# Mixer output projection: three weight chunks loaded and gated ahead, LayerNorm in two fused steps, and a fixed VectorE order

## The chip, the core and the metric

One core of one Trainium2 chip runs the whole program. Its engines are TensorE (PE), with a separate row for its weight loads (PEld), VectorE (DVE), ScalarE (ACT), GpSimd (POOL) and SyncE (SP), which issues nearly all transfers. The metric is device microseconds for one execution of the program. Three executions of the kernel before took 984.68, 987.9 and 989.28 us; the median is 987.9 us. A difference under about 0.5%, some 5 us, can't be told from no change with a measurement of this kind.

## What is computed

One layer of a hybrid encoder on 512 tokens of 1024 channels, all in float32. The part that matters here is the seam between the token mixer and the feed-forward network:

```python
    merged = gates[:, :, 0] * y_a + gates[:, :, 1] * y_b + gates[:, :, 2] * y_c
    return merged @ w_o
    ...
        y = _token_mixer(h, ...)
        x = _layer_norm(ALPHA * x + gt_t[:, None, :] * y) * ln_t_g[l] + ln_t_b[l]
        h = _modulate(x, sh_f, sc_f)      # _layer_norm(x) * (1 + sc_f) + sh_f
        y = _conv_ffn(h, w_up[l], conv_w[l], conv_b[l], w_down[l])
        x = _layer_norm(ALPHA * x + gt_f[:, None, :] * y) * ln_f_g[l] + ln_f_b[l]
```

Between the product with `w_o` and the first product with `w_up` there are thus two LayerNorms, one after the other, each over the 1024 channels of a token. The first has a gain and a bias per channel; the second has the adaptive scale and shift. The products need float32 accuracy. The kernel gets it by writing each operand as a high part and a low part (`...h` and `...l`) and multiplying three times: low by high, high by low, high by high.

## The kernel before

Every weight chunk has to be split before TensorE can use it: ScalarE casts it to the high part, and VectorE subtracts that from the raw chunk for the low part. Activations are split the same way.

**Merges.** `merge(2, m)`, for m from 0 to 7, adds the last branch's product to the merged activations: 24 matmuls on PE, a product with the gate on DVE (`th`, L408), the addition on POOL (`mg`, L411), then ACT casts the high half (`mgh`, L1079) and DVE subtracts for the low half (`mgl`, L1080). A merged tile is free for other use once its `mgl` is made.

**Output projection** (`project_out`). The tokens lie in four tiles t of 128 rows and the 1024 output channels in two halves n of 512, so there are eight accumulators `pyo`. The contraction has eight chunks k of `w_o`, named `o0` to `o7`. Chunks 0 and 1 are streamed through all eight accumulators (L1127 to L1130). Chunks 2 to 7 are resident: `scaled_chunk` loads one, POOL multiplies both halves with the gate row `gt` (L1096), ACT casts (L1107) and DVE makes the low half (L1108); only then the matmuls (L106 to L108) go tile by tile, so that `pyo` of t = 0 is complete first. In all 192 matmuls of 512 columns.

**Between the products** (`after_mixer(t)`, called as tile t is complete). The input tile has been loaded into `xr`. DVE adds ALPHA times it to `pyo` (L1180) and takes statistics of each half (L1183) and their aggregate `mv` (L142). POOL makes the reciprocal deviation `rs` in three small steps (`pw` L130, `rs` L133 and L145). ACT applies mean and deviation (L1187), then POOL (half 0) and DVE (half 1) apply gain and bias in two steps each (L1193, L1194). That is the first LayerNorm. Then come statistics again (L1207, L142), the small steps on POOL, and ACT writes the normalized tile to `xr` (L1214). PE turns pairs of tiles (`pth`, L1226; tp = 0 is tokens 0 to 255, tp = 1 tokens 256 to 511), and `second_modulation` applies scale and shift and splits: `h2f` and an even `h2T..h` on ACT (L1234, L1243), an odd one on DVE (L1238), the low parts on DVE (L1246).

**First part of the up-projection** (`up_early`). Six chunks of `w_up` are split in advance (`early_split`, `early_low`: `uph`/`upl` and `wuph`/`wupl` at L1160 and L1166). Their products with tokens 0 to 255 (`pzu`, 256 columns, 144 matmuls) run first, then those with tokens 256 to 511 (144 more), and after that the loop over the other 38 chunks (L113 to L116).

**What sets the order.** The program is written with tile pools, which set the waits; a scheduler places each engine's instructions by its own timeline of the program, and each engine then runs its list strictly in that order. `tc.issue_after` adds an order that data don't need; before, it keeps some steps behind marked ones (`marks`, `after`).

## Time and profile before

| | us |
|---|---|
| three executions | 984.68, 987.9, 989.28 |
| the profiled execution | 988.41 |
| its span, first to last instruction | 986.6 |
| PE busy in the span | 961.1 |
| DVE, ACT, POOL busy | 594.0, 393.8, 311.3 |
| mean clock granted to TensorE | 0.991 of full |
| first `pyo` matmul, last `pyo` matmul | 556.38, 601.70 |
| first `pzu` matmul on tokens 0 to 255 | 610.84 |
| first `pzu` matmul of the loop over the other chunks | 650.58 |

The times of the last three rows count from the start of the span. In a row of the timeline stand the start, the duration, engine, line, operation, the tiles written and read, and how many instructions the row holds; brackets give the idle time of the engine just before and the instruction that ended it. Matmuls are pipelined, so the distance between two starts tells their cost and not the duration. In a row of stretches stand the busy time of PE, PEld, DVE, ACT and POOL with the number of instructions, the clock granted, the share of the DMA engines and GB/s.

### The profile page before, as it was taken

How to read it: one execution, taken by the hardware profiler on the slowest of the kernel's cores; microseconds unless marked ns; L12 is line 12 of the kernel's file. 1: busy time of each engine (PE TensorE's matmuls, PEld its weight loads, DVE VectorE, ACT ScalarE, POOL GpSimd, SP SyncE). 2: the span in 40 equal slices, each digit the busy share in tenths (PEclk: the TensorE clock that was granted, in tenths of full speed). 3: DMA queues.
4: the chain of work that ended last, by engine and by line, in shares of the span. 5: the costliest groups of instructions: out<-in, count | busy, mean ns of one | idle time of the engine just before them, and what ended most of it. 6: DMA issues, size and time to landing. Idle time of an engine off the chain costs nothing.

```text
span 986.6 us, 12263 instructions
## 1 busy us (share of the span) xinstructions
PE 961.1 (97%) x4566; PEld 805.5 (82%) x4566; DVE 594.0 (60%) x891; ACT 393.8 (40%) x658; POOL 311.3 (32%) x311
## 2 busy tenths in 40 slices
PE   8999999999999999999999997999999999999996
PEld 7878888888878888888888876988888888888885
DVE  6967556556685565655533577685565665632367
ACT  4574646543333322522332335464444444422121
POOL 3773111122350031200012746321111121755654
PEclk9999999999999999999999997999999999999999
DMA  9722112144445533363232471133433342343222
GB/s 339 275 67 77 36 54 81 35 132 157 133 128 186 181 123 98 128 224 107 64 107 86 125 259 43 44 128 107 129 107 128 109 145 88 113 123 107 85 86 86
DMA packets 45275, 119.20 MB, mean 121 GB/s; under 512 B 5280, under 2 KB 8736, under 8 KB 45216
## 3 DMA queue, kind: packets, MB, share of 16 engines
q1 hardware_dynamic: 44784, 118.25, 36.9%
q8 instruction: 36, 0.59, 0.3%
q10 hardware_dynamic: 432, 0.17, 0.1%
q14 instruction: 23, 0.19, 0.1%
HBM read 116.30 MB, written 2.10 MB: 120 GB/s over the span
## 4 chain that ended last, share of the span: by engine, by line
PE 79%; DVE 8%; DMA 4%; POOL 4%; ACT 2%; issue 2%; DVEq 0%; SPq 0%; POOLq 0%; ACTq 0%
PE pzu L114 7%; PE pzu L113 7%; PE pzu L116 7%; PE pg L113 4%; PE py L113 4%; PE pg L116 3%; PE pg L114 3%; PE py L114 3%; PE py L116 3%; PE pyd L1127 3%; PE pyd L1130 3%; PE pyd L1129 3%; PE pu L933 3%; PE pu L930 3%; PE pu L932 3%; DVE acc L295 3%
## 5 line engine op out<-in xcount | busy, mean ns | idle before, releaser
L93 DVE TENSOR_TENSOR wupl<-wup,wuph 128x1024 fp32r<-128x1024 f32 x38 | 48.3, 1272 | 71.2 <-PE pzu L116 45.3
L1096 POOL TENSOR_TENSOR d<-d,gtfb 128x512 f32<-128x512 f32 x44 | 73.6, 1694 | 38.3 <-DMA d<-in_wdn 35.9
L1369 POOL TENSOR_TENSOR zc<-zc 128x512 f32<-128x512 f32 x22 | 29.7, 1350 | 173.7 <-ACT zc L1368 130.8
L411 POOL TENSOR_TENSOR mg<-mg,th 128x512 f32<-128x512 f32 x16 | 31.3, 1958 | 144.2 <-DVE th L408 144.0
L1101 DVE TENSOR_TENSOR dl<-d,dh 128x1024 fp32r<-128x1024 f32 x18 | 29.5, 1636 | 55.6 <-PE pyd L1127 50.7
L92 ACT CAST wuph<-wup 128x1024 fp32r<-128x1024 f32 x38 | 39.9, 1050 | 46.5 <-PE pzu L114 46.5
L92 ACT CAST wbh<-wb 128x1024 fp32r<-128x1024 f32 x24 | 25.3, 1054 | 69.3 <-PE py L114 52.6
L93 DVE TENSOR_TENSOR wgl<-wg,wgh 128x1024 fp32r<-128x1024 f32 x22 | 27.0, 1229 | 41.5 <-ACT wgh L92 29.3
L810 DVE SCALAR_TENSOR_TENSOR ada<-adar,cact,ada 128x512 f32<-128x512 f32 x56 | 49.7, 917 | 0.8 <-DMA adar<-in_ada 0.8
L1100 ACT CAST dh<-d 128x1024 fp32r<-128x1024 f32 x18 | 19.0, 1053 | 62.5 <-PE pyd L1130 37.6
L1351 ACT ACTIVATE zc<-pzu,cols 128x512 f32<-128x512 f32 x44 | 34.2, 779 | 22.0 <-PE pzu L116 17.3
L92 ACT CAST wgh<-wg 128x1024 fp32r<-128x1024 f32 x22 | 23.3, 1057 | 38.9 <-PE pg L114 25.2
L93 DVE TENSOR_TENSOR wsgl<-wsg,wsgh 128x1024 fp32r<-128x1024 f32 x16 | 19.6, 1225 | 31.8 <-ACT wsgh L92 26.2
L93 DVE TENSOR_TENSOR wbl<-wb,wbh 128x1024 fp32r<-128x1024 f32 x24 | 30.5, 1269 | 9.7 <-ACT wbh L92 5.5
L92 ACT CAST wsgh<-wsg 128x1024 fp32r<-128x1024 f32 x16 | 16.9, 1053 | 48.7 <-PE pu L933 44.1
L1354 DVE SCALAR_TENSOR_TENSOR zc<-pzu,cols,zc 128x511 f32<-128x511 f32 x44 | 32.6, 743 | 3.9 <-ACT zc L1351 3.9
L731 POOL TENSOR_SCALAR pe<-pe,mx 128x128 f32<-128x128 f32 (+3 forms) x32 | 17.0, 534 | 56.2 <-DVE mx L730 55.8
L1358 DVE SCALAR_TENSOR_TENSOR zc<-pzu,cols,zc 128x510 f32<-128x510 f32 x44 | 32.6, 745 | 0.8
L1096 POOL TENSOR_TENSOR o<-o,gttb 128x512 f32<-128x512 f32 x16 | 26.4, 1674 | 16.6 <-DMA o<-in_wo 13.7
L1368 ACT ACTIVATE zc<-zc 128x512 f32<-128x512 f32 x22 | 13.9, 631 | 40.5 <-DVE zc L1358 40.4
L863 POOL TENSOR_TENSOR asum<-apad 128x527 f32<-128x527 f32 x8 | 12.2, 1519 | 55.4 <-ACT apad L858 29.3
L408 DVE SCALAR_TENSOR_TENSOR th<-th,py 128x512 f32<-128x512 f32 x16 | 11.0, 686 | 30.9 <-PE py L116 30.9
(1430 smaller groups left out, 3170.4 us busy)
## 6 DMA issues: line engine op xcount, KB each, us to landing
wup<-in_wup SPq DMA_DIRECT2D x44, 512.0 KB, 3.6
adar<-in_ada SPq DMA_DIRECT2D x64, 256.0 KB, 3.9
wb<-in_wb SPq DMA_DIRECT2D x24, 512.0 KB, 3.6
wg<-in_wg SPq DMA_DIRECT2D x22, 512.0 KB, 3.6
d<-in_wdn SPq DMA_DIRECT2D x22, 512.0 KB, 3.6
wsg<-in_wsg SPq DMA_DIRECT2D x16, 512.0 KB, 3.7
ada<-in_ada1p SPq DMA_DIRECT2D x24, 256.0 KB, 5.0
wa<-in_wa SPq DMA_DIRECT2D x8, 512.0 KB, 3.5
```

Of the source, the lines that this page charges most:

```text
L92: nc.scalar.copy(out=hi[:, :n], in_=raw[:, :n])
L93: ins = nc.vector.tensor_tensor(out=lo[:, :n], in0=raw[:, :n], in1=f(hi[:, :n]), op=ALU.subtract)
L113: nc.tensor.matmul(o, wh[:, c], xl[k], start=k == 0, stop=False)
L114: nc.tensor.matmul(o, wh[:, c], xh[k], start=False, stop=False)
L116: nc.tensor.matmul(o, wl[:, c], xh[k], start=False, stop=k == KT - 1)
L411: nc.gpsimd.tensor_tensor(out=merged[m], in0=merged[m], in1=th, op=ALU.add)
L810: nc.vector.scalar_tensor_tensor(out=acc[n], in0=src, scalar=cact[:, k : k + 1], in1=acc[n], op0=ALU.mult, op1=ALU.add,)
L1096: nc.gpsimd.tensor_tensor(out=raw[:, c], in0=raw[:, c], in1=gt[n], op=ALU.mult)
L1351: nc.scalar.activation(t, pz, AF.Identity, bias=cols[:, cc + 3 : cc + 4], scale=cols[:, cc + 2 : cc + 3])
L1354: nc.vector.scalar_tensor_tensor(out=t[:, 1:512], in0=pz[:, 0:511], scalar=cols[:, cc + 1 : cc + 2], in1=t[:, 1:512], op0=ALU.mult, op1=AL ...
L1358: nc.vector.scalar_tensor_tensor(out=t[:, 2:512], in0=pz[:, 0:510], scalar=cols[:, cc : cc + 1], in1=t[:, 2:512], op0=ALU.mult, op1=ALU.add,)
L1369: nc.gpsimd.tensor_tensor(out=val, in0=val, in1=gate, op=ALU.mult)
```

## The change

Four things are changed, all between the last merges and the first `pzu` matmuls for tokens 256 to 511.

1. Chunks `o2`, `o3` and `o4` no longer go through `scaled_chunk`'s load. They are loaded as six half tiles (`oraw`) of another pool, and POOL gates one half for each of the first six merges. In the order that the scheduler makes of it, POOL runs these six rows just ahead of its first `mg` addition of the last branch.
2. The input rows are loaded straight into the tiles `x1`, which take the places of the merged tiles as these come free, and all eight loads are issued before the projection; on SP they stand between the weight loads of the merges.
3. The first LayerNorm has two steps on DVE, each with two tensor inputs: `centre` is (x - mean) * gain and `scale` is (that) * rs + bias. The step on ACT and the four on POOL and DVE are gone. POOL still makes `rs`, now in two steps.
4. DVE's steps are chained one behind the other (`in_turn`), from the last low half of `w_o` to the splits for tokens 256 to 511. The low halves of the early `w_up` chunks have fixed places in that chain: chunks 0 to 2 ahead of the first residual, chunk 3 between `centre` and `scale` of t = 0, chunk 4 after the second statistics of t = 1, chunk 5 after those of t = 3. The turns for tokens 0 to 255 stand inside the projection's last matmuls, and for these tokens all high parts are made on ACT.

The diff, cut to its core:

```diff
@@ during the merges
+    o_raw = {}
+    for k in (2, 3, 4):
+        o_raw[k] = [pt_t(f"oraw{k}{n}") for n in range(2)]
+        for n in range(2):
+            nc.sync.dma_start(out=o_raw[k][n], in_=A["wo"][k, :, n * 512 : (n + 1) * 512])
     for m in range(KT):
         merge(2, m, sg_hi, sg_lo, th2.pop(m))
+        if m < 6:
+            raw = o_raw[2 + m // 2][m % 2]
+            nc.gpsimd.tensor_tensor(out=raw, in0=raw, in1=gt_t[m % 2], op=ALU.mult)
@@ project_out
+        if ready:
+            ready()
         for t in range(TT):
             for n in range(2):
                 for k in range(nk - resident, nk):
+                    for work, *args in inside.get((t, n, k), ()):
+                        work(*args)
                     step(t, n, k, ws[k])
             chain(t, acc[t])
@@ the steps between the products
+    def in_turn(work, *args):
+        with ExitStack() as order:
+            for ins in vector_order:
+                order.enter_context(tc.issue_after(ins))
+            vector_order[:] = [work(*args).ins]
+    def centre(t):
+        for n in range(2):
+            ins = nc.vector.scalar_tensor_tensor(
+                out=x1[t][n], in0=x1[t][n], scalar=mv_o[t][:, 0:1], in1=lntg[n],
+                op0=ALU.subtract, op1=ALU.mult,
+            )
+        return ins
+    def scale(t):
+        for n in range(2):
+            ins = nc.vector.scalar_tensor_tensor(
+                out=x1[t][n], in0=x1[t][n], scalar=rs_o[t][:, 0:1], in1=lntb[n],
+                op0=ALU.mult, op1=ALU.add,
+            )
+        return ins
-    def affine(t):
-        for n in range(2):
-            nc.scalar.activation(
-                x1[t][n], x1[t][n], AF.Identity, bias=rs_o[t][:, 1:2], scale=rs_o[t][:, 0:1]
-            )
-    def gain_bias(t):
-        for n, eng in ((0, nc.gpsimd), (1, nc.vector)):
-            eng.tensor_tensor(out=x1[t][n], in0=x1[t][n], in1=lntg[n], op=ALU.mult)
-            eng.tensor_tensor(out=x1[t][n], in0=x1[t][n], in1=lntb[n], op=ALU.add)
+    def weights_ready():
+        vector_order[:] = last_lo
+        for m in range(4):
+            early_split(m)
+        for m in range(3):
+            in_turn(early_low, m, nc.vector)
+    def norm_steps(t, *between):
+        in_turn(residual, t)
+        in_turn(centre, t)
+        for work in between:
+            in_turn(*work)
+        in_turn(scale, t)
     def after_mixer(t, py):
         py_o[t] = py
+        if t < 2:
+            norm_steps(t, *[(early_low, 3, nc.vector)][t:])
+            in_turn(second_stats, t)
+            second_norm(t)
         if t == 1:
+            early_split(4)
+            in_turn(early_low, 4, nc.vector)
         if t == 2:
+            norm_steps(2)
         if t == 3:
+            in_turn(second_modulation, 0, 0)
+            in_turn(second_stats, 2)
+            for jp in (1, 2, 3):
+                in_turn(second_modulation, 0, jp)
+            second_norm(2)
+            early_split(5)
+            norm_steps(3)
+            in_turn(second_stats, 3)
+            second_norm(3)
+            in_turn(early_low, 5, nc.vector)
+    for t in range(TT):
+        x1[t] = [m_t(f"x1_{t}{n}") for n in range(2)]
+        for n in range(2):
+            nc.sync.dma_start(
+                out=x1[t][n], in_=A["x"][t * P : (t + 1) * P, n * 512 : (n + 1) * 512]
+            )
+        {
+            (3, 0, KT - 2): [(turn, 0, 0), (turn, 0, 1)],
+            (3, 1, 3): [(turn, 0, 2)],
+            (3, 1, 5): [(turn, 0, 3)],
+        },
```

How the order moves is seen best at three places. The first is VectorE behind the last low half of `w_o`, that is, where the residual of tile 0 is formed. `x1_00` and `x1_01` are the two halves of tile 0, `x1_10` and `x1_11` those of tile 1, `x1_20` of tile 2; `sto` and `st` hold statistics; `wupl` and `upl` are low halves of early `w_up` chunks. Before:

```order
L1180 SCALAR_TENSOR_TENSOR x1_00_5274<-xr00_5270,pyo_5080 128x512
L1183 BN_STATS sto_5276<-x1_00_5274 128x6
L1180 SCALAR_TENSOR_TENSOR x1_01_5275<-xr01_5271,pyo_5081 128x512
L1180 SCALAR_TENSOR_TENSOR x1_10_5291<-xr10_5287,pyo_5082 128x512
L1166 TENSOR_TENSOR wupl_5310<-wup_5307,wuph_5309 128x512
L1183 BN_STATS sto_5276<-x1_01_5275 128x6
L1166 TENSOR_TENSOR wupl_5310<-wup_5307,wuph_5309 128x512
L1183 BN_STATS sto_5293<-x1_10_5291 128x6
L1180 SCALAR_TENSOR_TENSOR x1_11_5292<-xr11_5288,pyo_5083 128x512
L142 BN_AGGR mv_5298<-sto_5276 128x2
L1166 TENSOR_TENSOR wupl_5394<-wup_5391,wuph_5393 128x512 x2
```

Now:

```order
L1180 TENSOR_TENSOR wupl_5265<-wup_5262,wuph_5264 128x512 x2
L1196 SCALAR_TENSOR_TENSOR x1_00_5098<-x1_00_5098,pyo_5114 128x512
L1196 SCALAR_TENSOR_TENSOR x1_01_5099<-x1_01_5099,pyo_5115 128x512
L1199 BN_STATS sto_5316<-x1_00_5098 128x6
L1199 BN_STATS sto_5316<-x1_01_5099 128x6
L1201 BN_AGGR mv_5321<-sto_5316 128x2
L1208 SCALAR_TENSOR_TENSOR x1_00_5098<-x1_00_5098,mv_5321,lntg0_5074 128x512
L1208 SCALAR_TENSOR_TENSOR x1_01_5099<-x1_01_5099,mv_5321,lntg1_5076 128x512
L1180 TENSOR_TENSOR wupl_5271<-wup_5268,wuph_5270 128x512 x2
L1216 SCALAR_TENSOR_TENSOR x1_00_5098<-x1_00_5098,rs_5323,lntb0_5078 128x512
L1216 SCALAR_TENSOR_TENSOR x1_01_5099<-x1_01_5099,rs_5323,lntb1_5080 128x512
L153 BN_STATS st_5333<-x1_00_5098 128x6
```

Tiles 0 and 1 were interleaved and now follow each other; the low halves of chunk 2 stand ahead of the first residual, those of chunk 3 between `centre` and `scale`, and the gain and bias, which came later from three engines, are these four rows.

The second place is ScalarE ahead of the first split for the up-projection (`h2T0h`, made of the turned tile `pth`; `xr` is the tile that the second LayerNorm writes). Before:

```order
L1160 CAST wuph_5309<-wup_5307 128x512 x2
L1160 CAST wuph_5393<-wup_5391 128x512 x2
L1187 ACTIVATE x1_00_5274<-x1_00_5274,rs_5300 128x512
L1187 ACTIVATE x1_01_5275<-x1_01_5275,rs_5300 128x512
L1187 ACTIVATE x1_10_5291<-x1_10_5291,rs_5368 128x512
L1187 ACTIVATE x1_11_5292<-x1_11_5292,rs_5368 128x512
L1214 ACTIVATE xr00_5270<-x1_00_5274,rs_5384 128x512
L1214 ACTIVATE xr01_5271<-x1_01_5275,rs_5384 128x512
L1214 ACTIVATE xr10_5287<-x1_10_5291,rs_5447 128x512
L1214 ACTIVATE xr11_5288<-x1_11_5292,rs_5447 128x512
L1234 ACTIVATE h2f_5470<-pth_5465,shfc_3497,scfc_4400 128x256
L1243 ACTIVATE h2T0h_5064<-pth_5465,shfc_3497,scfc_4400 128x256
```

Now:

```order
L1174 CAST wuph_5264<-wup_5262 128x512 x2
L1174 CAST wuph_5270<-wup_5268 128x512 x2
L1229 ACTIVATE xr00_5343<-x1_00_5098,rs_5338 128x512
L1229 ACTIVATE xr01_5344<-x1_01_5099,rs_5338 128x512
L1229 ACTIVATE xr10_5408<-x1_10_5102,rs_5403 128x512
L1229 ACTIVATE xr11_5409<-x1_11_5103,rs_5403 128x512
L1174 CAST uph40_5414<-wup_5412 128x512
L1174 CAST uph41_5415<-wup_5412 128x512
L1260 ACTIVATE h2T0h_5082<-pth_5485,shfc_3497,scfc_4400 128x256
L1263 ACTIVATE h2f_5529<-pth_5485,shfc_3497,scfc_4400 128x256
L1260 ACTIVATE h2T1h_5083<-pth_5485,shfc_3497,scfc_4400 128x256
```

The first LayerNorm's four rows (L1187) are gone, and the cast of `w_up` chunk 4 (`uph4`) stands between the second LayerNorm of tile 1 and the first split.

The third place is TensorE at the end of the projection: `pyo` are its accumulators, `pth` the turns, `pzu` the up-projection. Before:

```order
L106 MATMUL pyo_5087<-o7l1_5219,mgh7_5052 128x512
L107 MATMUL pyo_5087<-o7h1_5217,mgl7_5053 128x512
L108 MATMUL pyo_5087<-o7h1_5217,mgh7_5052 128x512
L1226 MATMUL pth_5465<-ident_95,xr00_5270 128x128
L1226 MATMUL pth_5483<-ident_95,xr00_5270 128x128
L1226 MATMUL pth_5495<-ident_95,xr01_5271 128x128
L1226 MATMUL pth_5554<-ident_95,xr01_5271 128x128
L1226 MATMUL pth_5465<-ident_95,xr10_5287 128x128
L1226 MATMUL pth_5465<-ident_95,xr00_5270 128x128
...
L106 MATMUL pzu_5616<-h2T0l_5072,uph00_5262 128x256
L107 MATMUL pzu_5616<-h2T0h_5064,upl00_5264 128x256
```

Now:

```order
L108 MATMUL pyo_5120<-o5h0_5214,mgh5_5002 128x512
L1241 MATMUL pth_5485<-ident_95,xr00_5343 128x128
L1241 MATMUL pth_5490<-ident_95,xr00_5343 128x128
L106 MATMUL pyo_5120<-o6l0_5228,mgh6_5039 128x512
...
L106 MATMUL pyo_5121<-o5l1_5217,mgh5_5002 128x512
L1241 MATMUL pth_5485<-ident_95,xr10_5408 128x128
L1241 MATMUL pth_5485<-ident_95,xr00_5343 128x128
L1241 MATMUL pth_5485<-ident_95,xr10_5408 128x128
...
L108 MATMUL pyo_5121<-o7h1_5239,mgh7_5070 128x512
L106 MATMUL pzu_5610<-h2T0l_5090,uph00_5248 128x256
L107 MATMUL pzu_5610<-h2T0h_5082,upl00_5250 128x256
```

The sixteen turns for tokens 0 to 255 stood behind the last `pyo` matmul and now stand inside tile 3's matmuls; twelve of them, which need tile 1's `xr10` and `xr11`, stand ahead of the projection's last eight.

More of the change, by code (lines that the diff above doesn't have):

```diff
@@ L1171, in residual_in, with second_stats, second_norm @@
+    def second_stats(t):
+        rs_o[t] = ln_stats(x1[t])
+        return aggregated[0]
+    def second_norm(t):
         xr[t] = [act_t(f"xr{t}{n}", F32) for n in range(2)]
         for n in range(2):
-            nc.sync.dma_start(
-                out=xr[t][n], in_=A["x"][t * P : (t + 1) * P, n * 512 : (n + 1) * 512]
-            )
-        x1[t] = [m_t(f"x1_{t}{n}") for n in range(2)]
-        st_o[t] = sm.tile([P, 2, 6], F32, name="sto", tag="sto")
-    def residual(t, n):
-        nc.vector.scalar_tensor_tensor(
-            out=x1[t][n], in0=xr[t][n], scalar=ALPHA, in1=py_o[t][n], op0=ALU.mult, op1=ALU.add
-        )
-        nc.vector.bn_stats(out=st_o[t][:, n, :], in_=x1[t][n])
@@ L1204, in second_stats @@
[L1204 to L1220 removed]
+            nc.scalar.activation(
+                xr[t][n], x1[t][n], AF.Identity, bias=rs_o[t][:, 1:2], scale=rs_o[t][:, 0:1]
+            )
@@ L1328, in trunk @@
     up_early((2, 3), 0)
-    for jp in (0,):
-        second_modulation(1, jp)
-    up_early((4, 5), 0)
-    for jp in (1, 2, 3):
-        second_modulation(1, jp)
+    up_early((4, 5), 0, 6)
+    for jp in range(4):
+        if jp:
+            turn(1, jp)
+        in_turn(second_modulation, 1, jp)
     a_hi = []
@@ L1344, in trunk @@
             else:
-                with after(3) if m < NE + 2 else ExitStack():
-                    uh, ul = wsplit(A["wup"][m], D, "wup")
+                uh, ul = wsplit(A["wup"][m], D, "wup")
                 pz = ps("pzu")
```

156 lines of the change are left out of this document (56 added, 100 removed).

## The prediction

> **What bounds the kernel now.** I read the page's shares first, then the chain of waits, then TensorE's timeline at the seam, then the rows before it on VectorE, ScalarE and POOL.
>
> ```profile
> PE 961.1 (97%) x4566; PEld 805.5 (82%) x4566; DVE 594.0 (60%) x891; ACT 393.8 (40%) x658; POOL 311.3 (32%) x311
> ```
>
> TensorE is busy 97% of the span, and the change takes no matmul away. So it can only win what TensorE loses now by waiting or by a low clock between the first `pyo` matmul and the loop that follows the early up-projection. TensorE's timeline there:
>
> ```profile
> 556.38 0.39 PE L1129 MATMUL pyo<-oh,mgh 128*128 128x512 f32 x1
> 601.47 0.39 PE L107 MATMUL pyo<-o7h,mgl 128*128 128x512 f32 x1
> 601.70 0.39 PE L108 MATMUL pyo<-o7h,mgh 128*128 128x512 f32 x1
> 605.80 1.40 PE L1226 MATMUL pth<-ident,xr 128*128 128x128 f32 x4 [3.71 <-ACT xr L1214]
> 608.37 2.82 PE L1226 MATMUL pth<-ident,xr 128*128 128x128 f32 x12 [1.17 <-ACT xr L1214]
> 610.84 0.58 PE L106 MATMUL pzu<-h2T0l,uph 128*128 128x256 f32 x1
> 650.58 0.40 PE L113 MATMUL pzu<-h2T0l,wuph 128*128 128x512 f32 x1
> ```
>
> Two losses are seen. The projection's 192 matmuls at 0.227 (601.47 to 601.70) would take 43.5 us; from 556.38 to 601.93 they take 45.55, so 2.0 is lost waiting for weights. Then 8.9 us pass until the first `pzu`, with 16 turns in them, behind the tile `xr`. The stretches show what the gap does to the clock (columns: PE, PEld, DVE, ACT, POOL busy, then the clock):
>
> ```profile
> 604.00:604.50 0.50, 0.00 (x0) 0.00 (x0) 0.50 (x2) 0.00 (x0) 0.50 (x2) 0.66 0.00 0
> 601.90:610.84 8.94, 4.03 (x17) 3.01 (x16) 5.52 (x13) 4.57 (x8) 5.76 (x13) 0.63 0.00 0
> 610.84:614.40 3.56, 3.56 (x18) 3.56 (x17) 3.10 (x4) 3.56 (x8) 2.75 (x2) 0.50 0.00 0
> 632.20:650.58 18.38, 18.38 (x156) 18.38 (x155) 11.63 (x22) 11.11 (x19) 0.00 (x0) 1.00 0.13 38
> ```
>
> The clock falls to half some 2.2 us after the last matmul and is still half over the first 3.56 us of `pzu`. Behind 632.2 TensorE runs dense: 18.38 us for the second half. The chain of waits names what makes `xr` late:
>
> ```profile
> 602.21 0.70 DVE x L1194
> 607.22 0.26 POOL rs L145
> 607.50 0.82 ACT xr L1214
> ```
>
> It is a chain of small steps over VectorE, POOL and ScalarE, not TensorE. I therefore follow the new order step by step on the clock of this execution and ask when the first `pzu` starts, and when the second half can.
>
> **The weights.** The rows of VectorE, ScalarE and the transfers at the projection's start:
>
> ```profile
> 568.96 1.28 DVE L1108 TENSOR_TENSOR o4l<-o,o4h 128x512 fp32r<-128x512 f32 x2
> 572.86 2.93 DVE L1108 TENSOR_TENSOR o5l<-o,o5h 128x512 fp32r<-128x512 f32 x2 [2.63 <-ACT o5h L1107]
> 582.01 0.68 DVE L1108 TENSOR_TENSOR o7l<-o,o7h 128x512 fp32r<-128x512 f32 x1
> 584.03 0.69 DVE L1180 SCALAR_TENSOR_TENSOR x<-xr,pyo 128x512 f32<-128x512 f32 x1 [1.34 <-PE pyo L108]
> 588.09 1.15 ACT L1160 CAST wuph<-wup 128x512 fp32r<-128x512 f32 x2 [4.15 <-DMA wup<-in_wup]
> ```
>
> ```profile
> 563.73 0.69 DVE L1080 SCALAR_TENSOR_TENSOR mgl<-mg,mgh 128x512 fp32r<-128x512 f32 x1 [3.09 <-ACT mgh L1079]
> ```
>
> ```profile
> 564.53 3.36 POOL L1096 TENSOR_TENSOR o<-o,gttb 128x512 f32<-128x512 f32 x2 [1.49 <-DVE mgl L1080]
> ```
>
> `o2` to `o4` are ready by 570.2 as now. `o5` waits for its load and for POOL, which gates four more halves from 564 on. With six halves gated ahead and the load buffers of `o2` to `o4` free for `o5` to `o7`, the POOL row at 564.53 is the last gating, so VectorE goes on without a wait: from 568.96 eight subtractions 0.60 apart (two are 1.28 long, so 0.68 and a pitch of 0.60) end at 573.8, where `o7l` now ends at 582.7. TensorE's 2.0 us of waits go. The six gatings, their loads and the eight loads of x move into the last gates and merges. On SP each x load waits for the `mgl` of the merged tile whose place it takes, and the weight loads of the next merges are queued behind it; the last one waits for `mgl7` (563.73), with the six `w_up` loads behind, the first of them needed near 573. I cost them at nothing, since TensorE has its own work there and the merges' loads are issued well ahead of use; if that cover fails, the first `pyo` is late by up to one landing, 3.6 us by the next rows.
>
> Next on VectorE stand the low halves of `w_up` chunks 0 to 2. Their loads are priced by these rows of the page and of the chain:
>
> ```profile
> wup<-in_wup SPq DMA_DIRECT2D x44, 512.0 KB, 3.6
> 582.11 5.88 DMA wup<-in_wup
> ```
>
> The third takes a buffer that `o7l` frees at 573.8, lands at 577.4 with 3.6 us, is cast (0.6 for the half that VectorE needs first) and subtracted (two, 1.2): the first residual starts at 579.4 instead of 584.0. A landing of 5.9 us, as in the crowded stretch now, would cost 2.3 more. I take 3.6, because the x loads that crowd it now are gone from there.
>
> **The steps of one tile.** Durations come from these rows, the last three from the final LayerNorm, which has the same two fused steps:
>
> ```profile
> 585.36 1.41 DVE L1180 SCALAR_TENSOR_TENSOR x<-xr,pyo 128x512 f32<-128x512 f32 x2
> 591.74 0.20 DVE L142 BATCH_NORM_AGGREGATE mv<-sto 128x2 f32<-128x12 f32 x1
> 591.86 1.24 DVE L1166 TENSOR_TENSOR wupl<-wup,wuph 128x512 fp32r<-128x512 f32 x2
> 593.01 0.69 DVE L1183 BATCH_NORM_STATS2 sto<-x 128x6 f32<-128x512 f32 x1
> 593.62 0.67 DVE L1180 SCALAR_TENSOR_TENSOR x<-xr,pyo 128x512 f32<-128x512 f32 x1
> 979.63 0.21 DVE L1390 BATCH_NORM_AGGREGATE mv<-st 128x2 f32<-128x12 f32 x1
> 979.87 1.42 DVE L1394 SCALAR_TENSOR_TENSOR out<-out,mv,lnfg 128x512 f32<-128x512 f32 x2
> 981.73 1.61 DVE L1406 SCALAR_TENSOR_TENSOR out<-out,rs,lnfb 128x512 f32<-128x512 f32 x2 [0.44 <-POOL rs L133]
> ```
>
> Two residuals 1.41, two statistics 0.61 each, the aggregate 0.12 to 0.24: 2.8. `centre` 1.4. Then a wait of 0.44 for `rs`, or, in tile 0, chunk 3's low halves (1.2). `scale` 1.3. Second statistics 1.4. Tile 0 takes 8.1 us, to 587.5; tile 1 takes 7.3, to 594.8. What follows goes over POOL and ScalarE:
>
> ```profile
> 592.03 0.51 POOL L130 TENSOR_SCALAR pw<-mv 128x1 f32<-128x1 f32 x1 [5.93 <-DVE mv L142]
> 592.63 0.88 POOL L133 TENSOR_TENSOR rs<-pw,neghalf 128x1 f32<-128x1 f32 x1
> 593.91 1.52 ACT L1187 ACTIVATE x<-x,rs 128x512 f32<-128x512 f32 x2 [2.05 <-POOL rs L145]
> 579.32 1.14 ACT L1160 CAST uph<-wup 128x512 fp32r<-128x512 f32 x2
> ```
>
> From the aggregate's start (591.74) to ScalarE's step (593.91) are 2.17 us. So `xr10` starts at 594.6 + 2.17 = 596.8, and `xr11` ends at 598.2. TensorE, with 184 of 192 projection matmuls and four turns done at 556.38 + 42.2 = 598.6, hardly waits for them and ends the projection with all 16 turns near 601.7 (16 at 0.11 in place of the lost 2.0). ScalarE then casts `uph4` (first half 598.2 to 598.8), and VectorE, idle since 594.8, subtracts its halves to 600.0. That is the place where I see the new order give time away: residual, `centre`, wait and `scale` of tile 2 take 5.9 more, to 605.9, and only then comes `h2T0l`:
>
> ```profile
> 610.36 0.43 DVE L1246 TENSOR_TENSOR h2T0l<-h2f,h2T0h 128x256 fp32r<-128x256 f32 x1 [3.25 <-ACT h2T0h L1243]
> 631.83 0.42 DVE L1246 TENSOR_TENSOR h2T0l<-h2f,h2T0h 128x256 fp32r<-128x256 f32 x1 [5.12 <-ACT h2T0h L1243]
> ```
>
> So the first `pzu` starts near 606.4 against 610.84, 4.4 earlier, and TensorE idles 4.7 us ahead of it. That gap is longer than the 2.2 us after which the clock fell, so the half clock stays.
>
> **The second half.** `h2T0l`, `h2T1l` and tile 2's statistics put its aggregate at 608.0 and `xr2` at 610.2 to 611.6; ScalarE then casts `uph5` (1.1) and makes the last two splits of tokens 0 to 255, so `h2T7l` ends at 615.0. Tile 3 takes 5.9 to 620.9, its statistics start the aggregate at 622.1, `xr3` runs from 624.3 to 625.7, the turn and the first split take 1.8: `h2T0l` of tokens 256 to 511 near 627.5, against 632.2 now. TensorE by its own work: 606.4 + 144 x 0.118 (18.38 over 156) + 8 turns = 624.3, and the low clock adds between 1.8 (half of 3.56) and 3.0 (half of the dense work from 608.37 to 614.40): 626.1 to 627.3. Chain and TensorE meet, and the chain is a little later. From 632.2 to 650.58 are 18.4 us now, unchanged. The loop then starts near 645.8 instead of 650.6. **The sum: 4.8 us less**, 988.41 - 4.8 = 983.6 in the profiled execution, and 983.1 on the scale of the runs, whose median is 0.5 below it. Its own range, from the two landings and one more wait of 0.5 in each tile, is a gain of 2.5 to 7, or 981 to 985.5.
>
> **The rivals.** *TensorE hardly waits.* If the steps are as short as the shortest rows and the clock is kept, the floor is 556.38 + 43.5 + 32 turns (3.6) + 288 x 0.118 = 637.5, a gain of 13.1: 974.8, and up to 980 with part of the gap. For it speaks that ScalarE is nearly empty; against it, that the chain as summed puts `h2T0l` at 605.9 whatever TensorE does.
>
> *No gain.* VectorE is now held by POOL's small steps. Rows that bear on it: where POOL multiplies whole tiles (564.53), VectorE's two-input subtractions run long:
>
> ```profile
> 564.34 2.39 DVE L1108 TENSOR_TENSOR o2l<-o,o2h 128x512 fp32r<-128x512 f32 x2
> ```
>
> That is 2.39 for two against 1.28 at 568.96, when POOL is quiet. If the small steps held `centre` and `scale` likewise, each of the four LayerNorms would lose `pw` and `rs`, 0.51 + 0.88 = 1.39, in all 5.6: 983.1 + 5.6 = 988.7. Against it: the two subtractions at 591.86 took 1.24 while `pw` and `rs` ran beside them. The Trainium skill has this as a rule on the page "SBUF — State Buffer", section "Who interferes with whom": a VectorE instruction with two SBUF inputs contends with a GpSimd one that reads SBUF, through a shared port that is locked. The trace agrees for the large gatings and not for the small steps. A landing of 5.9 us and a late `uph4` end in the same place, 985.5 to 988.7.
>
> *Slower.* The clock stays at half. TensorE starts `pzu` from a longer rest than now, without the turns that now run 2.5 us ahead of it, and a fixed VectorE order lets it run dry again at each tile. At half clock a matmul of 256 columns takes twice 0.118; if none of the first 144 gets the full clock, they end 144 x 0.118 = 17.0 us later than undisturbed, at 641.3 instead of 624.3, and the loop starts at 659.7: 9.1 later than now, 997. It is slower than now from the point where more than 67 of the 144 run at half clock (67 x 0.118 = 7.9, from 624.3 to 632.2). Against it: the low halves come 0.43 apart, faster than TensorE uses them, so between 606.4 and 614 it runs dense, and in the rows above dense work from 608.37 brought the clock back at 614.4. The Trainium skill, page "TensorE: Matmul & The Clock Gate", section "What's actually happening", puts the return to full speed after one busy window of about 3.4 us, in windows that run freely; by that rule the low clock ends within two windows, the loss is at most 3.4 us, and this rival falls. The trace's 6.0 us of dense work agrees.
>
> **How the numbers follow.** Forecast as summed: 0.62. TensorE hardly waits: 0.12. No gain: 0.18. Slower: 0.08. The time is 983.1. The range 978.5 to 988.8 holds the forecast, the case without a gain and a little of the fast one, and leaves out 0.18. A measurement here tells about 0.5%, or 4.9 us, from no change; that bound, 983.0, cuts the forecast nearly in half. Faster: 0.31 of the forecast and 0.12 = 0.43; slower: 0.08 less a little = 0.07; the same: 0.50.
>
> **What would show it.** Right: `o7l` ends near 574; the first residual near 579.4; no wait of PE on `o..l`; two fused steps of 1.4 each with 0.4 between; VectorE idle some 4 us ahead of `upl4`; first `pzu` near 606.4 behind `h2T0l` with the clock at 0.5; `h2T0l` for the second half near 627.5; loop at 645.8. Wrong: residual 0 waiting for a `wup` landing beyond 4 us; `centre` or `scale` well over 0.7 each; a wait on SP in the merges, so that the first `pyo` is later than 556.4; the clock at full in the gap, or at half beyond 612.

## The result and the profile after

The changed kernel takes 981.71 us (median of 12 executions, 979.05 to 984.64); the kernel before takes 986.91 us (median of 12, 984.68 to 990.0). The ratio is 0.9949, with a 95% interval from 0.9937 to 0.9961: about 5 us faster, right at the bound of what was called no change.

The two profiled executions differ by more, 988.41 against 979.05 us. TensorE reaches the projection at 556.38 us in the one and at 552.91 in the other, and this point moves from execution to execution: a second profile of the changed kernel has it at 555.09, and the kernels below, which have nearly the same work ahead of the seam, anywhere from 553.58 to 557.41. I therefore measure the seam by itself, from the first `pyo` matmul to the first matmul of the up-projection's loop, and call this **the stretch**: 94.20 us before (650.58 - 556.38), 88.25 us now. TensorE's timeline of the changed kernel:

```profile
552.91 0.39 PE L1137 MATMUL pyo<-oh,mgh 128*128 128x512 f32 x1
595.15 1.47 PE L1241 MATMUL pth<-ident,xr 128*128 128x128 f32 x12
598.08 0.39 PE L108 MATMUL pyo<-o7h,mgh 128*128 128x512 f32 x1
602.61 0.38 PE L106 MATMUL pzu<-h2T0l,uph 128*128 128x256 f32 x1 [4.14 <-DVE h2T0l L1269]
622.91 0.39 PE L106 MATMUL pzu<-h2T0l,uph 128*128 128x256 f32 x1 [0.39 <-DVE h2T0l L1269]
641.16 0.40 PE L113 MATMUL pzu<-h2T0l,wuph 128*128 128x512 f32 x1
```

The projection takes 45.2 us with 16 turns in it, where it took 45.3 without them: the 2 us of waits on weights are gone. The gap behind it is 4.3 us and no longer 8.9, and TensorE rests in it once, for VectorE's `h2T0l`, and no longer twice for `xr`. VectorE's rows show the chain that the prediction followed:

```profile
569.33 1.28 DVE L1115 TENSOR_TENSOR o7l<-o,o7h 128x512 fp32r<-128x512 f32 x2
572.53 1.29 DVE L1180 TENSOR_TENSOR upl<-wup,uph 128x512 fp32r<-128x512 f32 x2 [1.91 <-ACT uph L1174]
577.12 1.28 DVE L1196 SCALAR_TENSOR_TENSOR x<-x,pyo 128x512 f32<-128x512 f32 x2
579.88 1.42 DVE L1208 SCALAR_TENSOR_TENSOR x<-x,mv,lntg 128x512 f32<-128x512 f32 x2
589.26 1.40 DVE L1216 SCALAR_TENSOR_TENSOR x<-x,rs,lntb 128x512 f32<-128x512 f32 x2
591.90 0.21 DVE L142 BATCH_NORM_AGGREGATE mv<-st 128x2 f32<-128x12 f32 x1
595.49 1.29 DVE L1180 TENSOR_TENSOR upl<-wup,uph 128x512 fp32r<-128x512 f32 x2 [3.38 <-ACT uph L1174]
602.14 0.41 DVE L1269 TENSOR_TENSOR h2T0l<-h2f,h2T0h 128x256 fp32r<-128x256 f32 x1
609.29 0.43 DVE L1269 TENSOR_TENSOR h2T6l<-h2f,h2T6h 128x256 fp32r<-128x256 f32 x1 [3.67 <-ACT h2f L1263]
622.44 0.42 DVE L1269 TENSOR_TENSOR h2T0l<-h2f,h2T0h 128x256 fp32r<-128x256 f32 x1
```

In brackets stand VectorE's two long rests: 3.38 us ahead of the low halves of `w_up` chunk 4, and 3.67 ahead of `h2T6l`. Both end with ScalarE, whose rows say why (`uph` at 594.86 is chunk 4, at 607.22 chunk 5):

```profile
593.42 1.52 ACT L1229 ACTIVATE xr<-x,rs 128x512 f32<-128x512 f32 x2 [5.31 <-POOL rs L145]
594.86 1.12 ACT L1174 CAST uph<-wup 128x512 fp32r<-128x512 f32 x2
605.79 1.52 ACT L1229 ACTIVATE xr<-x,rs 128x512 f32<-128x512 f32 x2 [4.34 <-POOL rs L145]
607.22 1.13 ACT L1174 CAST uph<-wup 128x512 fp32r<-128x512 f32 x2
```

ScalarE itself rested 5.31 us and then 4.34 us, in its fixed order, in front of a second LayerNorm (tile 1, then tile 2). What VectorE needed stands behind it: first the cast of chunk 4, then the last splits of tokens 0 to 255, which come after one more cast. The clock (seventh figure) in four half microseconds:

```profile
602.50:603.00 0.50, 0.39 (x3) 0.40 (x4) 0.50 (x3) 0.00 (x0) 0.00 (x0) 1.00 0.00 0
603.00:603.50 0.50, 0.50 (x5) 0.50 (x5) 0.50 (x2) 0.00 (x0) 0.00 (x0) 0.60 0.00 0
606.00:606.50 0.50, 0.50 (x4) 0.50 (x4) 0.00 (x0) 0.50 (x1) 0.00 (x0) 0.50 0.00 0
606.50:607.00 0.50, 0.50 (x6) 0.50 (x6) 0.00 (x0) 0.50 (x2) 0.00 (x0) 0.99 0.00 0
```

It falls only when TensorE is already at work again (near 603.1) and is half for some 3.4 us, which at half speed is an estimated 1.7 us of work lost.

### The profile page after: what moved, and what is told of

Same layout as the page of the kernel before. It is cut to its first block, busy times and chain, and to the rows that moved or that the text cites. A ratio compares the mean times of both kernels' runs of the same rounds, so it can differ in the third digit from the quotient of the medians.

```text
span 977.2 us, 12237 instructions
## 1 busy us (share of the span) xinstructions
PE 957.4 (98%) x4566; PEld 805.0 (82%) x4566; DVE 588.8 (60%) x899; ACT 388.8 (40%) x654; POOL 291.1 (30%) x295
## 4 chain that ended last, share of the span: by engine, by line
PE 85%; DVE 5%; POOL 4%; ACT 2%; issue 2%; DMA 2%; DVEq 0%; POOLq 0%; SPq 0%
PE pzu L113 7%; PE pzu L114 7%; PE pzu L116 7%; PE pg L113 4%; PE py L113 4%; PE pg L114 4%; PE pg L116 4%; PE py L114 4%; PE py L116 4%; PE pyd L1138 3%; PE pyd L1135 3%; PE pyd L1137 3%; PE pu L932 3%; PE pu L931 3%; PE pu L929 3%; PE lat L508 2%
## 5 line engine op out<-in xcount | busy, mean ns | idle before, releaser
L410 POOL TENSOR_TENSOR mg<-mg,th 128x512 f32<-128x512 f32 x16 | 31.3, 1958 | 92.5 <-DVE th L407 92.4
L1385 ACT ACTIVATE zc<-zc 128x512 f32<-128x512 f32 x22 | 13.9, 631 | 40.5 <-DVE zc L1375 40.4
L294 DVE SCALAR_TENSOR_TENSOR acc<-ada,cact,acc 128x512 f32<-128x512 f32 (+1 forms) x27 | 26.9, 1011 | 0.7
```

The lines of the kernel that those rows point to most:

```text
L410: nc.gpsimd.tensor_tensor(out=merged[m], in0=merged[m], in1=th, op=ALU.add)
```

## The experiments

Times are medians; the ratio (below 1 is faster) is to the kernel before, run beside it on the same chip. "First early product" is the first `pzu` matmul and "second low part" the end of VectorE's `h2T0l` for tokens 256 to 511, both counted, like the stretch, in one profiled execution from its first `pyo` matmul. In the cuts of code, `...`, comments and words in parentheses stand for lines left out.

| kernel | us | ratio to before (95% interval) | first early product | second low part | stretch |
|---|---|---|---|---|---|
| before | 986.91 | 1 | 54.46 | 75.87 | 94.20 |
| the changed kernel | 981.71 | 0.9949 (0.9937 to 0.9961) | 49.70 | 69.95 | 88.25 |
| loads alone (`e1_loads_only`) | 984.55 | 0.997 (0.9956 to 0.9985) | 52.18 | 73.08 | 91.42 |
| all but the loads (`e2_order_only`) | 989.8 | 1.0031 (1.0017 to 1.0045) | 57.76 | 79.11 | 97.40 |
| fused steps undone (`e9_three_engines`) | 988.36 | 1.0012 (0.9999 to 1.0025) | 54.96 | 77.37 | 95.66 |
| turns put back (`e8_turns_behind`) | 981.73 | 0.9948 (0.9931 to 0.9964) | 49.74 | 69.97 | 88.26 |
| extra matmuls in the rest (`e4_warm`) | 981.1 | 0.9935 (0.9912 to 0.9958) | 50.31 | 71.04 | 89.35 |
| cast moved (`e3_cast_early`) | 977.66 | 0.9901 (0.9868 to 0.9934) | 46.18 | 66.91 | 85.21 |
| residual first (`e5_residual_first`) | 979.01 | 0.9925 (0.9909 to 0.9941) | 45.38 | 68.09 | 86.39 |
| cast moved, splits first (`e7_splits_first`) | 975.42 | 0.9887 (0.9873 to 0.9902) | 45.88 | 64.61 | 82.90 |
| residual first, splits first (`e6_both`) | 975.59 | 0.9893 (0.9878 to 0.9909) | 45.38 | 64.49 | 82.78 |

The last two columns differ by 18.3 us in every row: TensorE works off the second half in the same time, wherever it starts, so the question is always what makes the second low part late: the chain that leads to it, or TensorE itself, which has to reach the turn ahead of it. Which of the two it was shows at that turn: with extra matmuls, cast moved, residual first, both orders together and unfused steps TensorE waits there for `xr` (0.27 to 0.92 us), with the others it doesn't. My theory was a chain over VectorE, ScalarE and POOL; the rivals were TensorE's low clock, the loads by themselves, and a VectorE held by POOL.

### The early loads alone

```diff
 (the kernel before)
+    o_raw = {}   # chunks 2, 3, 4 as six half tiles, loaded ahead of the merges
     for m in range(KT):
         merge(2, m, sg_hi, sg_lo, th2.pop(m))
+        if m < 6:
+            raw = o_raw[2 + m // 2][m % 2]
+            nc.gpsimd.tensor_tensor(out=raw, in0=raw, in1=gt_t[m % 2], op=ALU.mult)
 ...  # scaled_chunk takes the gated halves of chunks 2, 3, 4 in place of a load
```

> The kernel before with the first part of the change alone: chunks o2 to o4 loaded as half tiles and gated ahead; the LayerNorm steps, the x loads and the order stay those of before. The stretch is counted from the first output-projection matmul to the first matmul of the up-projection's loop: 94.20 us before, 88.25 us in the changed kernel. Theory (weights early and fused steps are both needed, since between the projection and the up-projection a chain over VectorE, POOL and ScalarE ends last): the last low half of w_o ends some 18 us after the first projection matmul instead of 26, TensorE's 2.0 us of waits on weights go, but the five-step LayerNorm and the crowded w_up loads stay, so the stretch is 89.5 to 92.5 and the time 982.5 to 985.5. Rival (the loads alone bring the whole gain): stretch 88.3 or less, time near 981.5.

Measured: 984.55 us and a stretch of 91.42, as the theory had it. The last low half of `w_o` ends 18.0 us after the first `pyo` matmul (573.53 - 555.56), as in the changed kernel (17.7). But the gain stops at half, and TensorE's timeline shows where the rest stays:

```profile
598.15 0.44 PE L1234 MATMUL pth<-ident,xr 128*128 128x128 f32 x2 [3.16 <-ACT xr L1222]
605.62 1.58 PE L1234 MATMUL pth<-ident,xr 128*128 128x128 f32 x12 [0.68 <-ACT xr L1222]
607.74 0.39 PE L106 MATMUL pzu<-h2T0l,uph 128*128 128x256 f32 x1 [0.54 <-DVE h2T0l L1254]
```

It still waits for `xr`, now first inside the projection (3.16 us) and then behind it (0.68). The loads alone are not the whole gain.

### Everything but the early loads

```diff
 (the changed kernel)
-    o_raw = {}   # and its loads and gatings
-        o_raw, weights_ready,
+        {}, weights_ready,
```

> The changed kernel without its first part: all six resident chunks of w_o are loaded and gated as before; x loads, fused LayerNorm steps and the fixed VectorE order stay. Theory: the fixed order starts behind the last low half of w_o, so when that is late by the 8.6 us that it was (26.3 against 17.7 us after the first projection matmul), everything behind it is late by as much: stretch 96 to 97.5, which is 2 to 3 us longer than before, and time 989 to 991, slower than before. Rival (the fused steps bring a gain by themselves): stretch 91 to 93, time 984 to 986.

Measured: 989.8 us and a stretch of 97.40, as the theory had it: by 0.3%, with an interval that leaves out 1, slower than before. VectorE's rows:

```profile
580.83 0.69 DVE L1107 TENSOR_TENSOR o7l<-o,o7h 128x512 fp32r<-128x512 f32 x1 [0.37 <-ACT o7h L1106]
585.81 1.29 DVE L1172 TENSOR_TENSOR wupl<-wup,wuph 128x512 fp32r<-128x512 f32 x2 [1.40 <-ACT wuph L1166]
587.02 1.28 DVE L1188 SCALAR_TENSOR_TENSOR x<-x,pyo 128x512 f32<-128x512 f32 x2
```

The last `w_o` half ends at 581.52, 25.8 us after the first `pyo` matmul (555.74), and the first residual stands behind it and three more chunks, at 31.3 us instead of 24.2. This fixed order is only as early as its first link. The parts are not additive: the loads alone save 2.8 us of the stretch, the rest alone loses 3.2, together they save 6.0.

### The fused steps undone

```diff
 (the changed kernel)
-        in_turn(centre, t)
+        affine(t)                # ScalarE, after POOL's third step
         for work in between:
             in_turn(*work)
-        in_turn(scale, t)
+        in_turn(gain_bias, t)    # VectorE: two multiplications, two additions
```

> The changed kernel with the first LayerNorm's two fused steps taken apart again: POOL finishes the factors, ScalarE applies mean and deviation, VectorE multiplies by the gain and adds the bias in four steps (both halves on VectorE). The early loads, the x loads and the fixed VectorE order stay. Theory: from the aggregate to the end of the LayerNorm a tile takes 2.2 (to ScalarE) + 0.8 (its first half) + 2.7 (four steps on VectorE) = 5.7 us instead of the 3.4 measured with the fused steps, less 0.7 in tile 0 where chunk 3's low halves fill the gap; three such tiles lie ahead of the first early product and a fourth ahead of the second half, so the first early product comes 6 to 7 us later (55.7 to 56.7) and the stretch is 8 to 9.5 us longer: 96 to 98, time 989.5 to 991.5, slower than the kernel before. Rival (the fused steps matter little, VectorE's rests take up the difference): stretch 88 to 91, time below 985.

In the kernel before, POOL did the multiplication and the addition of half 0; here VectorE does both halves, so this is a LayerNorm in unfused steps and not quite the old one.

Measured: 988.36 us, a stretch of 95.66 and the first early product at 54.96 us. The sign and the mechanism are the theory's: against these unfused steps the fused ones are worth 7.4 us of the stretch. The size is short of its range, the stretch by 0.3 us, the first early product by 0.7, the time by 1.1. The reason lies largely on POOL, in these rows of tiles 0 and 1:

```profile
581.93 0.52 POOL L130 TENSOR_SCALAR pw<-mv 128x1 f32<-128x1 f32 x1 [15.32 <-DVE mv L1201]
582.53 0.88 POOL L133 TENSOR_TENSOR rs<-pw,neghalf 128x1 f32<-128x1 f32 x1
...
591.39 0.19 POOL L130 TENSOR_SCALAR pw<-mv 128x1 f32<-128x1 f32 x1 [1.40 <-DVE mv L1201]
591.67 0.55 POOL L133 TENSOR_TENSOR rs<-pw,neghalf 128x1 f32<-128x1 f32 x1
```

and in VectorE's beside them:

```profile
581.75 1.25 DVE L1180 TENSOR_TENSOR wupl<-wup,wuph 128x512 fp32r<-128x512 f32 x2
584.67 1.40 DVE L1218 TENSOR_TENSOR x<-x,lntg 128x512 f32<-128x512 f32 x2 [1.67 <-ACT x L1212]
...
591.10 0.21 DVE L1201 BATCH_NORM_AGGREGATE mv<-sto 128x2 f32<-128x12 f32 x1
593.47 1.40 DVE L1218 TENSOR_TENSOR x<-x,lntg 128x512 f32<-128x512 f32 x2 [2.16 <-ACT x L1212]
```

Beside two-input subtractions the two small steps take 0.52 and 0.88; with VectorE at rest they take 0.19 and 0.55. I had priced all tiles with the slow figure (2.2 us from aggregate to ScalarE). With VectorE waiting, as it does here in tiles 1 to 3, the way is 1.5 us: ScalarE starts at 592.62 behind the aggregate at 591.10.

### The turns put back behind the projection

```diff
 (the changed kernel)
-        { (3, 0, KT - 2): [(turn, 0, 0), (turn, 0, 1)], ... },
         if t == 3:
+            for jp in range(4):
+                turn(0, jp)
             in_turn(second_modulation, 0, 0)
```

> The changed kernel with the sixteen turns for tokens 0 to 255 put back behind the projection's last matmul. Theory: TensorE rests some 4 us there anyway, the turns fill 1.8 us of that rest, and the first low part waits for VectorE, not for the turns: first early product at 49.7 us, stretch 87.8 to 88.7, no difference in time (981 to 982.4). Rival (the place of the turns brings part of the gain): first early product and stretch 1 to 2 us later, time near 983.3.

Measured: 981.73 us and a stretch of 88.26, the changed kernel's to 0.01. The projection ends 1.9 us earlier (43.29 us after its start, against 45.17) and TensorE waits longer for the same row: the first early product comes at 49.74. In this kernel the place of the turns is worth nothing, since they only trade one rest for another.

### Extra matmuls in TensorE's rest

```diff
 (the changed kernel, in up_early)
+        for _ in range(warm):   # 18, ahead of the first two chunks' products alone
+            nc.tensor.matmul(pzs[ms[0]], mg_hi[7][:, :P], mg_hi[6], start=True, stop=True)
```

> The changed kernel with 18 extra matmuls of 512 columns (4.1 us) in TensorE's rest between the last projection matmul and the first early product; their sums are overwritten by the real product that follows, and nothing waits for them. They keep TensorE busy, so the clock should stay at full over the first early products. Theory (the VectorE chain of the second half ends at the same point as TensorE's own work, so there is nothing to win from the clock alone): clock 1.0 throughout, first early product at 49.7 us as now, stretch 87.7 to 88.4, time within 0.6 us of the changed kernel's 981.7. Rival (the half clock of TensorE sets the end): stretch 86.3 to 86.8, time near 980.

Measured: 981.1 us. The stretches with the clock (seventh figure):

```profile
599.70:604.60 4.90, 4.23 (x19) 3.18 (x17) 4.83 (x10) 3.75 (x9) 1.05 (x2) 1.00 0.36 107
604.60:608.00 3.40, 3.39 (x28) 3.39 (x29) 2.99 (x8) 0.21 (x1) 1.15 (x3) 1.00 0.00 0
612.00:624.00 12.00, 10.47 (x86) 10.03 (x85) 8.42 (x15) 2.20 (x5) 3.35 (x5) 1.00 0.12 38
```

The clock stays at full, and nothing is won: the time is within 0.6 us of the changed kernel's. TensorE has 1.5 us of waits later instead, in these two rows. Both are for the second chain, in which the low halves of chunk 5 (`upl`) stand behind tile 3's second statistics:

```profile
620.61 0.38 PE L107 MATMUL pzu<-h2T0h,upl 128*128 128x256 f32 x1 [1.00 <-DVE upl L1180]
622.84 0.87 PE L1241 MATMUL pth<-ident,xr 128*128 128x128 f32 x6 [0.53 <-ACT xr L1229]
```

The stretch of the profiled execution is 89.35, 0.95 above the theory's range and on the far side of the rival's 86.5: VectorE waited 0.44 us for `rs` in two tiles here and in none of the changed kernel's profile, so its chain was 1.1 us later. Even with the changed kernel's own chain the clock would win next to nothing: there ScalarE had the first half of tile 3's `xr` done at 620.28 and TensorE began the turn at 620.35, without a wait. The low clock does not end the seam by itself; it and the second chain end at the same point.

### One cast moved

```diff
 (the changed kernel)
     def weights_ready():
-        for m in range(4):
+        for m in range(5):
             early_split(m)
 ...
         if t == 1:
-            early_split(4)
             in_turn(early_low, 4, nc.vector)
```

> The changed kernel with one cast moved: ScalarE casts the early w_up chunk 4 right behind chunk 3 and no longer behind the second LayerNorm of tile 1, so that VectorE's low halves of chunk 4, which it waits for 3.4 us now, find their input ready. Nothing else changes. Theory (VectorE's chain sets the start of both halves of the early up-projection): VectorE's wait ahead of these low halves goes, the first early product starts some 3.5 us earlier (46.2 us after the first projection matmul instead of 49.7), TensorE rests under 1 us and keeps its clock, and the second half's first low part comes 3.5 earlier: stretch 84.5 to 85.2, time near 978.2. Rival (TensorE's half clock after the rest sets the end): the clock's 1.7 us come on top, stretch 83.0 to 83.5. Second rival (the loads or ScalarE hold the chain anyway): stretch within 0.5 of 88.25.

Measured: 977.66 us, first early product at 46.18 us, stretch 85.21, that is 3.04 less and at the upper edge of the theory's range. VectorE's rows at the place of the first long rest:

```profile
593.95 0.21 DVE L142 BATCH_NORM_AGGREGATE mv<-st 128x2 f32<-128x12 f32 x1
594.08 1.25 DVE L1180 TENSOR_TENSOR upl<-wup,uph 128x512 fp32r<-128x512 f32 x2
595.25 1.28 DVE L1196 SCALAR_TENSOR_TENSOR x<-x,pyo 128x512 f32<-128x512 f32 x2
```

The rest of 3.38 us is gone, and with it TensorE's half clock. The first early product is 3.5 us earlier, the whole stretch 3.0, not the 4.7 to 5.2 that the clock's rival asked for. Of the 0.5 between them, 0.44 is a wait of VectorE for `rs` in tile 3, which the changed kernel's profile doesn't have.

### The residual first

```diff
 (the changed kernel)
     def weights_ready():
-        for m in range(3):
-            in_turn(early_low, m, nc.vector)
 ...
-        if t < 2:
-            norm_steps(t, *[(early_low, 3, nc.vector)][t:])
+        if t < 3:
+            norm_steps(t, (early_low, t, nc.vector))
 ...  # chunk 3 behind h2T3l, chunk 4 inside tile 3's LayerNorm, chunk 5 ahead of its second statistics;
 ...  # early_split(4) now stands just ahead of second_norm(2)
```

> The changed kernel with the low halves of the early w_up chunks moved in VectorE's chain: tile 0's residual comes straight behind the last low half of w_o; the low halves of chunks 0, 1 and 2 stand between centre and scale of tiles 0, 1 and 2, chunk 3 behind the third low half of the up-projection's input, chunk 4 between centre and scale of tile 3, chunk 5 ahead of tile 3's second statistics. ScalarE still makes the last splits of tokens 0 to 255 behind the second LayerNorm of tile 2. Theory (two chains one behind the other): the first is ready when TensorE ends the projection, so the first early product comes at 45.3 to 46 us instead of 49.7; but the second, which waits for those last splits, moves only some 2.5 us: VectorE's first low part for tokens 256 to 511 ends at 67 to 68 us instead of 69.95, and the stretch is 85.3 to 86.5, time 978 to 979.5. Rival (only the start of the early products counts): stretch 82 to 83, time near 975.5.

Measured: 979.01 us, first early product at 45.38 us, stretch 86.39. TensorE goes from the projection to the early products without a rest, earlier than in any kernel so far, and yet the stretch is 1.2 us longer than with the moved cast alone. So the first chain is not what counts in the end: the second low part is, at 68.09 us, just beyond the theory's 67 to 68. It waits here, too, and the low halves of chunks 4 and 5, 1.2 us each, now stand inside tile 3's steps:

```profile
606.37 0.42 DVE L1269 TENSOR_TENSOR h2T6l<-h2f,h2T6h 128x256 fp32r<-128x256 f32 x1 [3.25 <-ACT h2f L1263]
```

### The last splits ahead of the second LayerNorm

```diff
 (the kernel with the moved cast)
-            second_norm(2)
-            early_split(5)
+            with tc.issue_after(last_full[0]):   # ScalarE's last h2f of tokens 0 to 255
+                second_norm(2)
+                early_split(5)
             norm_steps(3)
```

> The kernel of the moved cast (e3_cast_early) with one order added on ScalarE: the second LayerNorm of tile 2 and the cast of chunk 5 come behind the last splits of tokens 0 to 255 and no longer ahead of them. Nothing else changes. Theory: VectorE's wait of 3.7 us ahead of the last two low parts goes, tile 3's residual starts some 3.7 us earlier, so the second chain ends before TensorE's own work (144 products and 8 turns, 18.2 us behind the first early product at 46.2): TensorE then runs without a wait, and the stretch is 82.4 to 83.2, time 975 to 976. Rival (ScalarE's order is hidden behind TensorE): stretch 85.2 as with the moved cast alone, time 977.7.

Measured: 975.42 us and a stretch of 82.90. The second rest shrinks from 3.67 to 0.39 us (and 0.48, as before, one low part later), and tile 3's residual follows at once:

```profile
602.91 0.42 DVE L1271 TENSOR_TENSOR h2T6l<-h2f,h2T6h 128x256 fp32r<-128x256 f32 x1 [0.39 <-ACT h2f L1264]
603.82 0.42 DVE L1271 TENSOR_TENSOR h2T7l<-h2f,h2T7h 128x256 fp32r<-128x256 f32 x1 [0.48 <-ACT h2f L1264]
604.17 1.28 DVE L1196 SCALAR_TENSOR_TENSOR x<-x,pyo 128x512 f32<-128x512 f32 x2
```

The ratio's interval overlaps that of the moved cast alone, so that this second step gains is shown by the profiles and not by the times. TensorE is now dense from the first early product up to the second half, at the full clock, and ScalarE waits for TensorE's turn (1.68 us), where with the moved cast alone TensorE waited 0.53 us for ScalarE's `xr`:

```profile
599.50:603.00 3.50, 3.49 (x29) 3.49 (x30) 3.08 (x9) 3.50 (x9) 1.15 (x3) 1.00 0.00 0
603.00:617.00 14.00, 14.00 (x119) 14.00 (x119) 8.70 (x16) 5.44 (x10) 2.71 (x5) 1.00 0.14 39
```

```profile
616.30 0.56 ACT L1261 ACTIVATE h2T0h<-pth,shfc,scfc 128x256 fp32r<-128x256 f32 x1 [1.68 <-PE pth L1242]
```

From the first early product to the loop pass 37.0 us, against 38.55 in the changed kernel; the 1.5 us between them are about what the half clock was estimated to cost. In both, TensorE still rests once in this part, 0.4 us for the second low part itself.

### Both together, and the direct comparison

> The low halves moved as in e5_residual_first (chunk 5 behind tile 3's second statistics) and ScalarE's order as in e7_splits_first. Theory: both chains end before TensorE needs them; first early product at 45.3 to 46 us, stretch 81.7 to 82.5, TensorE's clock at full throughout, time 974.5 to 975.5. Rival (the loads of the early w_up chunks, which now follow one another behind each low half, hold ScalarE's casts and so the second LayerNorm): stretch 83.5 or more.

Measured: 975.59 us, first early product at 45.38, stretch 82.78, 0.3 above the theory's range. Its ratio and that of the kernel above can't be told apart. The first early product comes 0.5 us earlier, but TensorE waits 0.27 us at the later turn for `xr`: once TensorE is dense, an earlier first chain brings next to nothing.

The best kernel and the changed one were then run beside each other:

> The kernel of e7_splits_first once more, beside the changed kernel on one chip. Theory: the difference is that of the two stretches, 88.25 - 82.9 = 5.4 us; time 975 to 976.5. Rival (a part of the 6.3 us between the medians measured so far was chance, a part of the stretch's gain is given back behind it): 3 us or less.

> The changed kernel once more, beside the others on one chip. Theory: stretch 88.3 within 0.5, time 981 to 982.5. The stretch in the first profile may have been a lucky one, since the whole execution was 2.7 us under its median; by that rival it is 89.5 or more here.

Measured: 976.06 against 981.59 us, 5.5 apart, where the first profiles' stretches differ by 5.35. The changed kernel's stretch is 88.18 this time, so the first was no lucky one; the better kernel's is 83.85, 0.95 longer than in its first profile: the first residual came 0.43 us later, VectorE waited 0.44 for `rs` in tile 1, and TensorE, with its turns inside the projection, waited for both. So this time the stretches differ by 4.3 us where the medians differ by 5.5; single profiles can scatter by about a microsecond. Against the kernel before, the better one stands at 0.9898 (0.987 to 0.9926).

## Why the prediction was right

It foretold 983.1 us, 4.8 less than the 987.9 of the three executions known then. Measured were 981.7 and a ratio that means 5.0 us. Of the 1.4 us between the two times, 1.0 is the starting point: over twelve executions the kernel before has a median of 986.9. Step by step, in us from the first `pyo` matmul:

| step | forecast | measured |
|---|---|---|
| last low half of `w_o` ends | 17.4 | 17.7 |
| first residual starts | 23.0 | 24.2 |
| second LayerNorm of tile 1 starts on ScalarE | 40.4 | 40.5 |
| low halves of `w_up` chunk 4 start | 42.4 | 42.6 |
| first early product | 50.0 | 49.7 |
| `h2T7l` ends | 58.6 | 57.7 |
| second low part ends | 71.1 | 69.95 |
| loop starts | 89.4 | 88.25 |

- **The loads moved into the merges.** They were costed at nothing, and no cost shows: the first `pyo` matmul lies between 552.91 and 557.41 with them and at 556.38 and 555.74 in the two kernels without.
- **The weights.** Eight subtractions 0.60 apart without a wait: right. The third `w_up` landing was mis-sized, 4.53 us in the chain of waits where 3.6 was taken; the bound of 5.9 covered it.
- **The tiles.** Tile 0 took 8.06 us against 8.1, tile 1 6.84 against 7.3. The wait of 0.44 for `rs` did not come in that execution, which was luck: it did in others (the last section says when).
- **The way over POOL.** 2.17 us were taken from aggregate to ScalarE; 1.52 were measured (591.90 to 593.42), where VectorE rested and POOL's first two steps took 0.19 and 0.55 instead of 0.51 and 0.88. This and the missing wait gave back what the landing cost: the chain was 1.2 us late at the first residual, 0.8 at tile 1's last aggregate and 0.1 at ScalarE's step. So the first early product fitted to 0.3 us by errors that cancel.
- **The place that gives time away.** VectorE's rest ahead of chunk 4's low halves was named and sized at 4.0 us (594.8 to 598.8); it was 3.4. With the moved cast the stretch is 3.0 us shorter.
- **The clock.** The forecast had it at half from the first early product on, because the rest is longer than the 2.2 us after which it fell before. It was at full there and fell 0.5 us later, 4.8 us after the last projection matmul. The loss was half of 3.4 us and not of 3.56, so this term's size fits although its time was wrong.
- **The second half.** Chain and TensorE's own work were to meet, with the chain a little later. They met within 0.1 us, as the turn at 620.35 shows. Here the forecast was 1.2 us too slow: the 0.44 for `rs` was missing in tiles 2 and 3 as well, the way over POOL took 1.67 us in tile 2 and not 2.17, and the low parts follow each other 0.34 us apart and not 0.43.
- **What it didn't see.** The second rest, of 3.67 us ahead of `h2T6l`, was inside the sum ("ScalarE then casts `uph5` and makes the last two splits") but not named as a loss. It was longer than the first. Without it the stretch is 2.3 us shorter (85.21 - 82.90) by the better kernel's first profile and 1.4 by its second; the moved cast's profile has two waits of 0.44 for `rs`, these two have none and one.

Of the rivals, *TensorE hardly waits* failed on the two rests of VectorE, and comes near once both are gone: 82.9 us against its floor of 81.1 (637.5 - 556.4). *No gain* asked that POOL's small steps hold `centre` and `scale`. They don't, by more than a few hundredths: two `centre` steps took 1.42 us at 579.88 in tile 0 and 1.44 at 587.90 in tile 1, against 1.40 for two `scale` steps at 589.26 with POOL idle. Beside `centre` ran the first two rows in tile 0 and the last two in tile 1, beside the residual the two between:

```profile
579.94 0.74 POOL L130 TENSOR_SCALAR pw<-mv 128x1 f32<-128x1 f32 x1 [15.29 <-DVE mv L1201]
580.76 0.94 POOL L133 TENSOR_TENSOR rs<-pw,neghalf 128x1 f32<-128x1 f32 x1
585.36 0.19 POOL L130 TENSOR_SCALAR pw<-mv 128x1 f32<-128x1 f32 x1 [3.65 <-DVE mv L142]
585.63 0.56 POOL L133 TENSOR_TENSOR rs<-pw,neghalf 128x1 f32<-128x1 f32 x1
587.95 0.19 POOL L130 TENSOR_SCALAR pw<-mv 128x1 f32<-128x1 f32 x1 [1.39 <-DVE mv L1201]
588.23 0.86 POOL L133 TENSOR_TENSOR rs<-pw,neghalf 128x1 f32<-128x1 f32 x1
```

*Slower*, with the clock at half for the whole first half, did not come: the clock was back after 3.4 us at half, 3.9 us after the first early product. The Trainium skill's page "TensorE: Matmul & The Clock Gate" (section "What's actually happening") has it come back after one busy window of about 3.4 us; the trace agrees.

The stretch is 6.0 us shorter, the medians lie 5.2 us apart. The 0.8 us are not given back behind the seam: from the loop's first matmul to the end of the span pass 336.02 us before (986.6 - 650.58) and 336.04 now (977.2 - 641.16). What else differs from execution to execution is the stretch, by up to a microsecond, and the point where it starts, which moves by up to 4.5 us; whether the change itself moves it by less than a microsecond, no run here tells.

## What to carry to other kernels

When a seam between two dense stretches of TensorE is bound by a chain of small steps, lay the chain out once with the durations of rows and look for every place where the chain's engine rests: both gains left in this kernel were a cast or splits on ScalarE, which itself rested, that stood in the wrong place of its fixed order, and moving them won about as much again as the change itself (5.5 us after 5.2). A fixed order has to begin with something that is ready early; without the early loads the same order made this kernel slower. Moves that only filled a rest (the turns, the extra matmuls) were worth nothing here, because what ended the rest stayed where it was.
